# One stream of peer_u for the dense blocks of both passes, and a sixth block gathered wholly

## The chip, the cores and the metric

The kernel runs on one core of one Trainium2 chip: TensorE (PE), VectorE (DVE), ScalarE (ACT), GpSimd (POOL) and SyncE (SP), each with its own program, worked off in order, and 16 DMA engines that they share. The metric is the device time of one execution in microseconds.

## The reference

One layer of a decoder, sequence 1024, width 1024, float32. A token mixer (a gated linear recurrence and a causal convolution, merged and projected) comes first, then the part that the change touches, a product-key expert layer: each token picks 8 x 16 of 16384 experts, expert e being one row of `peer_u` and one of `peer_v`.

```
q = (hf @ w_q).reshape(T, PEER_HEADS, 2, PEER_DQ // 2)
s = jnp.einsum('thpd,hpnd->thpn', q, sub_keys)
sc, idx = lax.top_k(s, PEER_TOPK)
cand = sc[:, :, 0, :, None] + sc[:, :, 1, None, :]          # 256 sums a head
top_sc, pos = lax.top_k(cand, PEER_TOPK)                     # eidx = i * 128 + j of these
gate = jax.nn.softmax(top_sc)
act = gelu(einsum('thkd,td->thk', u_tab[eidx], h))
y = einsum('thk,thkd->td', gate * act, v_tab[eidx])
```

The result is `rms_norm(h + g2 * y)` with a last gain.

## The kernel before

The 1024 tokens are eight blocks of 128. The mixer works on two chunks of four blocks. After a chunk, `ask` makes its queries and top lists, and the expert layer treats its blocks in one of two ways.

*Dense.* All 128 groups of 128 experts are streamed, one group a step. `dots` (L1070) multiplies the group's rows of `peer_u` with the tokens' features into one PSUM tile "ups" and takes gelu of it into `act`; `weigh` (L1088) multiplies that by the dense weights `wgrp`; `add` (L1097) multiplies the weighted result with the group's rows of `peer_v` and sums in six PSUM tiles "y" over all steps. Both tables are float32 and every product is made of three exact ones: `split` (L300) makes a high part on ScalarE (uhi, vhi, whi, L301) and a rest on VectorE (ulo, vlo, wlo, L302). In a step `dots` issues 24 matrix products, and `add` six of 512 columns for each block. Before a block can be weighted densely, `spread` (L960) must build its weights: 128 pairs of one-hot rows and placing products (L982), written to the DRAM tensor `wd`.

*Gathered.* `gather_u` (L925) fetches for each of a token's 128 experts its row of `peer_u` by an indirect DMA on GpSimd's queue (L921, 128 rows, one for each token), and VectorE multiplies and sums it with the tokens' features (L937). `gather_v` (L944) fetches the rows of `peer_v` and VectorE accumulates them (L953). The rows land in tiles "gt": two buffers at first, five once the selection of the last blocks is done.

There are two passes of 128 steps, so each table is streamed twice. Pass one treats blocks 0, 1 and 2; pass two treats blocks 4 and 5 densely and block 6 by halves, its dots gathered and its sum dense. Blocks 3 and 7 are gathered wholly.

The order of the work is made in two ways. `Side` (L82) emits a few steps of the selection (`pick`) and of the gathers at each `tick()`, at rates set by constants; a tick stands after every quarter of `dots` and after each block of `add`. Then a scheduler places each engine's instructions by priority and by its own estimate of times. All loads and stores but the gathers go through SP's queue in that order. A tile pool with `bufs` buffers makes a new tile wait until the one `bufs` before it has been read: `uraw` has two, `vraw` three, "ups" one.

The dense part runs from the first product of `dots` (1616 us) to the last steps in `close` (L1122).

Of the kernel before, what the change touches and what calls it, by code (L numbers as in the profile page):

```python
# [31 lines left out]
PASSES = [([0, 1, 2], 3), ([4, 5, 6], 2)]  # L32
WIDE = 3
DENSE = [b for bs, nu in PASSES for b in bs[:nu]]
MIXED = [b for bs, nu in PASSES for b in bs[nu:]]
GATHERED = [3, 7]
# [5 lines left out]
RATE_GATHER = 0.25  # L42
RATE_PICK_END = 1.1
RATE_GATHER_END = 0.1
HASTE = 1.1
HASTE_LAST = 1.06
HASTE_PICK = 1.2
# [14 lines left out]
GAT_MORE = 3  # L62
VRAW = 3
# [18 lines left out]
class Side:  # L82
    """Work emitted a few steps at a time between the steps of other work, and how urgent it is beside that."""
# [38 lines left out]
def layer_kernel(tc, a, out):  # L122
# [18 lines left out]
    def tick():  # L141
        """A step of the work beside, its vector instructions kept behind the main work of a few steps ago."""
# [21 lines left out]
    with ctx:  # L164
# [41 lines left out]
        def rstd_of(ssq, n, scale, tag):  # L206
            """1 / sqrt(scale * ssq + EPS): a first guess from the exponent, then Newton steps."""
# [13 lines left out]
        # lower bounds of the forget gates  # L221
# [18 lines left out]
        def ada(js, cols=None):  # L240
            """Parts js of the conditioning: as rows in DRAM, or with features on the partitions of cols."""
# [62 lines left out]
        def transpose_split(pp, src, hi, lo, b):  # L304
            """src [tokens, features] -> token block b of hi, lo [feature, k, tokens]."""
# [14 lines left out]
        wd = dram.tile([S // TG, P, NKEYS, TG], F32, name="wd")  # L320

        GQ, GF, GI, GG, GCA, GCB, GGA, GGB = range(8)

        class Mm:
            """Products with streamed weights, 256 columns at a time, in two halves of the contraction."""
# [38 lines left out]
            def weights(self, name, i):  # L364
                """The planned weights that come next; those after them are made ready a product later."""
# [7 lines left out]
            def mm3(self, ps, l, r, step):  # L373
                """ps = sum over k of l(part, k)^T r(part, k) in three exact-product passes."""
# [10 lines left out]
            def feat(self, w, m, act):  # L385
                """Output features 128 m.. on partitions, tokens free."""
# [6 lines left out]
            def halves(self, w, act):  # L393
                """As feat for both m, the first half of the tokens first."""
# [7 lines left out]
            def tok(self, ws, bs, act):  # L402
                """Tokens of block b on partitions, 256 output features, for (w, b) of ws, bs."""
# [617 lines left out]
        def gather():  # L1021
# [4 lines left out]
            for _ in v:  # L1026
                yield
                if picked.keys() >= set(MIXED):
                    break
# [314 lines left out]
```

## Time and profile before

| | |
|---|---|
| three executions | 3749.34, 3755.42, 3763.02 us (median 3755.42) |
| span of the profiled execution, first to last instruction | 3746.1 us (its own time is not listed apart from the span) |
| PE, DVE, ACT, POOL busy | 3610.6 (96%), 3157.9 (84%), 1849.1 (49%), 779.3 us (21%) |
| DMA | 999.44 MB, mean 267 GB/s |
| chain that ended last | PE "y" 4% on each of three lines, "ups" 3% on each of three, others 1% or less |
| pass one | 1616 to 2799 us |
| pass two | 2799 to 3722 us |

Busy time of TensorE counts each matrix product from its start to a modelled end, and products overlap; how fast it works is seen from start to start in the timeline. A share of the DMA engines is the mean over 16 of them. Times in the rows below are from the span's start.

### The profile page before, as it was taken

The numbers are of one execution on the slowest core, as the hardware profiler recorded it, in microseconds if no ns is written. First come the engines' busy times: TensorE is split into PE (matmuls) and PEld (weight loads), VectorE is DVE, ScalarE is ACT, GpSimd is POOL, SyncE is SP. The second block draws the span as 40 slices with busy tenths as digits, with TensorE's granted clock in tenths as the row PEclk, the third lists the DMA queues.
The fourth block names the chain that finished last, engine by engine and source line by source line (L and its number), as shares of the span: only waits on it lengthen the run. The fifth ranks groups of instructions, "written<-read, shape, count | busy, mean of one in ns | idle before, by whom it ended". The sixth has DMA issues, their size and how long they took to land. (4 is left out here: it accounts for less than half of the span.)

```text
span 3746.1 us, 57252 instructions
## 1 busy us (share of the span) xinstructions
PE 3610.6 (96%) x20610; PEld 3203.6 (86%) x20610; DVE 3157.9 (84%) x6739; ACT 1849.1 (49%) x3260; POOL 779.3 (21%) x652
## 2 busy tenths in 40 slices
PE   8999999899999999999999999999998999999997
PEld 5888888778899879988888899999987888888886
DVE  4999989967899966789898888898888888778888
ACT  4111355523467877644444566666534444444443
POOL 0000000000000100013333434343333333233332
PEclk9999999899999999999999999999999999999999
DMA  5222477468444778778788999999999999999996
GB/s 230 79 79 90 152 257 258 168 211 316 164 144 152 241 279 318 270 264 285 261 275 287 345 324 330 332 344 355 332 328 327 328 333 344 316 330 340 328 340 214
DMA packets 371405, 999.44 MB, mean 267 GB/s; under 512 B 30376, under 2 KB 142504, under 8 KB 360112
## 3 DMA queue, kind: packets, MB, share of 16 engines
q1 hardware_dynamic: 278960, 660.19, 50.5%
q0 software_dynamic: 92160, 335.59, 25.3%
q8 instruction: 162, 2.65, 0.3%
q14 instruction: 123, 1.01, 0.1%
HBM read 864.57 MB, written 131.09 MB: 266 GB/s over the span
## 5 line engine op out<-in xcount | busy, mean ns | idle before, releaser
L921 POOL DMA_INDIRECT gt<-in_peer_u_dram,ei x384 | 465.2, 1211 | 2139.1 <-ACT o L759 947.2
L1078 PE MATMUL ups<-u,uhi 128*128 128x384 f32 (+1 forms) x2048 | 637.8, 311 | 12.8 <-ACT act L1086 12.8
L1079 PE MATMUL ups<-u,uhi 128*128 128x384 f32 (+1 forms) x2048 | 636.2, 311 | 2.4 <-DMA u<-u2s 2.4
L1080 PE MATMUL ups<-u,ulo 128*128 128x384 f32 (+1 forms) x2048 | 635.9, 311 | 0.0
L1108 PE MATMUL y<-vhi,whi 128*128 128x512 f32 x1524 | 587.0, 394 | 12.0 <-ACT whi L301 8.0
L1109 PE MATMUL y<-vlo,whi 128*128 128x512 f32 x1524 | 589.9, 393 | 1.6 <-DVE vlo L302 1.5
L937 DVE SCALAR_TENSOR_TENSOR gt<-gt,ut 128x1024 f32<-128x1024 f32 x384 | 466.3, 1219 | 63.9 <-DMA gt<-in_peer_u_dram,ei 58.6
L1112 PE MATMUL y<-vhi,wlo 128*128 128x512 f32 x1524 | 465.7, 392 | 5.9 <-DVE wlo L302 5.9
L301 ACT ACTIVATE uhi<-uraw 128x512 fp32r<-128x512 f32 x512 | 309.9, 625 | 227.0 <-PE ups L1079 177.5
L921 POOL DMA_INDIRECT gt<-in_peer_v_dram,ei x256 | 313.1, 1223 | 515.5 <-DVE yg L953 459.9
L1078 PEld LDWEIGHTS ups<-u,uhi 128*128 128x128 f32 x2048 | 390.0, 190 | 25.6 <-ACT act L1086 16.1
L302 DVE TENSOR_TENSOR ulo<-uraw,uhi 128x512 fp32r<-128x512 f32 x512 | 346.0, 687 | 78.0 <-ACT uhi L301 76.1
L302 DVE TENSOR_TENSOR vlo<-vraw,vhi 128x1024 fp32r<-128x1024 f32 x256 | 312.8, 1222 | 110.8 <-ACT vhi L301 109.8
L1079 PEld LDWEIGHTS ups<-u,uhi 128*128 128x128 f32 x2048 | 390.1, 190 | 12.3 <-DMA u<-u2s 3.1
L1080 PEld LDWEIGHTS ups<-u,ulo 128*128 128x128 f32 x2048 | 389.8, 190 | 0.3
L301 ACT ACTIVATE vhi<-vraw 128x1024 fp32r<-128x1024 f32 x256 | 270.2, 1056 | 234.7 <-PE y L1112 140.7
L1108 PEld LDWEIGHTS y<-vhi,whi 128*128 128x128 f32 x1524 | 287.3, 189 | 68.6 <-ACT whi L301 11.4
L1112 PEld LDWEIGHTS y<-vhi,wlo 128*128 128x128 f32 x1524 | 284.9, 188 | 69.3 <-DVE wlo L302 11.0
L1109 PEld LDWEIGHTS y<-vlo,whi 128*128 128x128 f32 x1524 | 286.4, 189 | 55.2 <-DVE vlo L302 2.4
L953 DVE SCALAR_TENSOR_TENSOR yg<-gt,gate,yg 128x1024 f32<-128x1024 f32 x254 | 324.7, 1278 | 5.6 <-DMA gt<-in_peer_v_dram,ei 5.4
L301 ACT ACTIVATE whi<-wgrp 128x384 fp32r<-128x384 f32 x256 | 133.7, 522 | 352.4 <-DVE wgrp L1091 315.7
L469 DVE SCALAR_TENSOR_TENSOR y<-gl,convw,y 128x1024 f32<-128x1024 f32 x240 | 292.8, 1277 | 0.3
(298 smaller groups left out, 7460.9 us busy)
## 6 DMA issues: line engine op xcount, KB each, us to landing
uraw<-in_peer_uT_dram SPq DMA_DIRECT2D x256, 512.0 KB, 6.4
vraw<-in_peer_v_dram SPq DMA_DIRECT2D x256, 512.0 KB, 6.1
raw<-in_w_in_dram SPq DMA_DIRECT2D x96, 512.0 KB, 5.0
wd<-wt SPq DMA_DIRECT2D x48, 1024.0 KB, 6.7
wgrp<-wd SPq DMA_DIRECT2D x32, 1536.0 KB, 14.0
adaw<-in_ada_w_dram SPq DMA_DIRECT2D x24, 1024.0 KB, 8.1
raw<-in_wq_dram SPq DMA_DIRECT2D x32, 512.0 KB, 5.2
raw<-in_w_b_dram SPq DMA_DIRECT2D x16, 512.0 KB, 4.3
```

What stands on the lines that cost most here:

```text
L301: nc.scalar.activation(hi, src, AF.Copy)
L302: nc.vector.tensor_sub(lo, src, hi.bitcast(F32))
L469: nc.vector.scalar_tensor_tensor(ys[0], gl[:, j:j + S], convw[:, cb, j:j + 1], ys[0], op0=OP.mult, op1=OP.add)
L921: nc.gpsimd.indirect_dma_start(out=gt, out_offset=None, in_=a[table], in_offset=bass.IndirectOffsetOnAxis(ap=ei[:, j:j + 1], axis=0))
L937: nc.vector.scalar_tensor_tensor(gt, gt, 1.0, ut, op0=OP.mult, op1=OP.mult, accum_out=act[:, j:j + 1])
L953: nc.vector.scalar_tensor_tensor(y, gt, w[:, j:j + 1], y, op0=OP.mult, op1=OP.add)
L1078: nc.tensor.matmul(o, hi[:, k], u2[kh][:, 0, k, :m], start=kh + k == 0, stop=False)
L1079: nc.tensor.matmul(o, hi[:, k], u2[kh][:, 1, k, :m], start=False, stop=False)
L1080: nc.tensor.matmul(o, lo[:, k], u2[kh][:, 0, k, :m], start=False, stop=kh + k == 4)
L1108: nc.tensor.matmul(ys[x][dh], whi[:, r], vhi[:, c], start=first, stop=False)
L1109: nc.tensor.matmul(ys[x][dh], whi[:, r], vlo[:, c], start=False, stop=False)
L1112: nc.tensor.matmul(ys[x][dh], wlo[:, r], vhi[:, c], start=False, stop=last)
```

## The change

`peer_u` is streamed once. In each step of pass one, `dots` runs for the blocks of the first pass and again, with the same cut rows, for the blocks of the second; the gelu of the latter goes to the DRAM tensor `ad`, and pass two reads it back, eight steps at a time, as `agrp`. Pass two treats blocks 4 and 5 alone. Block 6 joins 3 and 7 as wholly gathered. The gathers may begin before the other blocks of the chunk are selected, at higher rates; their later buffers are two and two in place of two and three, and `vraw` has two buffers in place of three.

```diff
-PASSES = [([0, 1, 2], 3), ([4, 5, 6], 2)]
+PASSES = [[0, 1, 2], [4, 5]]
-GATHERED = [3, 7]
+GATHERED = [3, 6, 7]
+TICKS = [11, 2]
+LAST_STEPS = 40
-RATE_GATHER = 0.25
+RATE_GATHER = 0.35
-RATE_GATHER_END = 0.1
+RATE_GATHER_END = 0.25
-HASTE_LAST = 1.06
-HASTE_PICK = 1.2
+HASTE_PICK = 2.0
-GAT_MORE = 3
-VRAW = 3
+GAT_MORE = 2
+VRAW = 2
...
+        ad = dram.tile([NKEYS, P, P * len(PASSES[1])], F32, name="ad")
...
+                if not c:
+                    gats.append(ctx.enter_context(tile_pool(name="gat0", bufs=GAT_BUFS, side="right")))
-                for b in sorted(blocks, key=lambda b: (b not in MIXED, b not in GATHERED or c, b)):
+                for b in sorted(blocks, key=lambda b: (b != GATHERED[c], b)):
...
-                if s < end:
+                if s < NKEYS:
                     cut_u[s, kh] = cut(up, raw_u[s][:, 4 * kh:4 * kh + 4], "u", [P, 4, P], 4)
...
-            def dots(s):
+            def dots(s, p):
+                m, off = sizes[p], p * sizes[0]
                 ps = ups.tile([P, n], F32, name="ups")
...
-                acts[s] = dp.tile([P, n // TG, TG], F32, name="act", bufs=AHEAD + 2)
-                nc.scalar.activation(acts[s][:, :m // TG], ps[:, :m].rearrange("p (b t) -> p b t", t=TG), AF.Gelu)
+                if p == 0:
+                    acts[s] = dp.tile([P, n], F32, name="act", bufs=AHEAD + 2)
+                    nc.scalar.activation(acts[s], ps, AF.Gelu)
+                else:
+                    t = dp.tile([P, m], F32, name="actb")
+                    nc.scalar.activation(t, ps[:, :m], AF.Gelu)
+                    nc.sync.dma_start(ad[s], t)
+
+            def kept_acts(s):
+                i = s % NKEYS
+                ag[s // IGRP] = late[0].tile([P, IGRP, sizes[1]], F32, name="agrp")
+                nc.sync.dma_start(ag[s // IGRP], ad[i:i + IGRP].rearrange("i p t -> p i t"))
...
+                act = ag[s // IGRP][:, s % IGRP] if p else acts.pop(s)
+                nc.vector.tensor_mul(w, w, act.rearrange("p (b t) -> p b t", t=TG))
...
+                    gathers[1] = (left - LAST_STEPS) / (TICKS[0] * (NKEYS - 4)) * HASTE if s < 0 else (
+                        left / (TICKS[1] * (NKEYS - 8)) * HASTE)
...
+                if s == NKEYS:
+                    upc.close()
+                    late.append(upc.enter_context(tile_pool(name="bp", bufs=2)))
+                    kept_acts(s)
                 j = s + 4
-                if 0 <= j < end:
+                if 0 <= j < NKEYS:
                     raw_u[j] = up.tile([P, KB, P], F32, name="uraw", bufs=2)
...
-                    dots(s)
+                if 0 <= s < NKEYS:
+                    dots(s, 0)
                 if 0 <= s - AHEAD < end:
                     weigh(s - AHEAD)
-                if 0 <= s - lag < end - 2:
-                    add(s - lag)
+                if blocks and 0 <= s < NKEYS:
+                    add(j, blocks[:2])
+                    blocks = blocks[2:]
+                if 0 <= s < NKEYS:
+                    dots(s, 1)
+                if blocks:
+                    add(j, blocks)
```

In the changed file the products of `dots` stand on L1075 to L1077, those of `add` on L1121, L1122 and L1125, the splits on L300 and L301, the weighing on L1102 and the second gather's sum on L952.

TensorE in the middle of pass one, before. The rows are the end of one step's `dots`, into the PSUM tile ups_20803, and what follows it.

```order
L1078 MATMUL ups_20803<-u21_15345,uhi_20634 128x384
L1079 MATMUL ups_20803<-u21_15345,uhi_20634 128x384
L1080 MATMUL ups_20803<-u21_15345,ulo_20635 128x384
L1108 MATMUL y00_15661<-vhi_21002,whi_20973 128x512
L1109 MATMUL y00_15661<-vlo_21003,whi_20973 128x512
L1108 MATMUL y01_15662<-vhi_21002,whi_20973 128x512
L1109 MATMUL y01_15662<-vlo_21003,whi_20973 128x512
```

TensorE in the middle of pass one of the changed kernel: ups_26082 holds the dots of the first pass's blocks (384 columns), ups_26135 those of the second pass's (256), both in the one buffer.

```order
L1075 MATMUL ups_26082<-u21_15501,uhi_25946 128x384
L1076 MATMUL ups_26082<-u21_15501,uhi_25946 128x384
L1077 MATMUL ups_26082<-u21_15501,ulo_25947 128x384
L1075 MATMUL ups_26135<-u20_15496,uhi_25927 128x256
L1076 MATMUL ups_26135<-u20_15496,uhi_25927 128x256
L1077 MATMUL ups_26135<-u20_15496,ulo_25928 128x256
L1075 MATMUL ups_26135<-u20_15496,uhi_25927 128x256
```

Where the products of `add` followed before, the second 24 of `dots` now follow the first 24, in 98 of the 128 steps; the 18 products of `add` then come after both. In 28 other steps 12 or 6 products of `add` stand between.

VectorE in pass two, before. One step's vlo to the next one's: gt are gathered rows, ulo and wlo rests of splits.

```order
L302 TENSOR_TENSOR vlo_30391<-vraw_30242,vhi_30390 128x1024
L937 SCALAR_TENSOR_TENSOR gt_29716,act_27726<-gt_29716,ut_27724 128x1024
L1091 TENSOR_TENSOR wgrp_29797<-wgrp_29797,act_30212 128x16x16
L302 TENSOR_TENSOR ulo_30190<-uraw_30018,uhi_30189 128x512
L937 SCALAR_TENSOR_TENSOR gt_30237,act_27726<-gt_30237,ut_27724 128x1024
L302 TENSOR_TENSOR ulo_30206<-uraw_30018,uhi_30205 128x512
L302 TENSOR_TENSOR wlo_30360<-wgrp_29797,whi_30359 128x384
L302 TENSOR_TENSOR vlo_30466<-vraw_30314,vhi_30465 128x1024
```

VectorE in the first half of pass two of the changed kernel, the same stretch.

```order
L301 TENSOR_TENSOR vlo_31953<-vraw_31904,vhi_31952 128x1024
L301 TENSOR_TENSOR wlo_31981<-wgrp_31712,whi_31980 128x256
L952 SCALAR_TENSOR_TENSOR yg_28274<-gt_29327,gate7_19444,yg_28274 128x1024
L952 SCALAR_TENSOR_TENSOR yg_28274<-gt_29336,gate7_19444,yg_28274 128x1024
L301 TENSOR_TENSOR wlo_32004<-wgrp_31712,whi_32003 128x256
L301 TENSOR_TENSOR vlo_31976<-vraw_31927,vhi_31975 128x1024
L952 SCALAR_TENSOR_TENSOR yg_28274<-gt_29351,gate7_19444,yg_28274 128x1024
L952 SCALAR_TENSOR_TENSOR yg_28274<-gt_29373,gate7_19444,yg_28274 128x1024
L301 TENSOR_TENSOR wlo_32027<-wgrp_31712,whi_32026 128x256
```

The two ulo of each step are gone, and the weighing stands there for eight steps at once (L1102 ... x8, or in two parts, every eighth step, not in these rows). Two gathered rows stand between one vlo and the next, up to the 56th step of pass two; after it there are none.

## Rows read from the trace of the kernel before

**Rows 1.** Windows: us, busy us (instructions) by engine, clock, DMA share, GB/s

```profile
1240.00:1510.00 270.00, 247.49 (x1664) 227.06 (x1663) 193.51 (x505) 207.59 (x477) 20.59 (x20) 0.96 0.82 287
...
1616.00:2799.00 1183.00, 1155.59 (x6130) 1050.70 (x6129) 1025.90 (x2131) 641.99 (x1254) 428.31 (x345) 1.00 0.90 316
2799.00:3722.00 923.00, 904.87 (x5392) 807.13 (x5391) 757.51 (x1105) 389.75 (x649) 320.12 (x266) 0.99 0.93 327
2800.00:3000.00 200.00, 186.46 (x1089) 164.34 (x1088) 163.38 (x286) 80.78 (x137) 68.18 (x54) 0.98 0.94 332
```

**Rows 2.** Timeline of TensorE, pass one: start us, duration us, what

```profile
2002.16 0.33 PE L1078 MATMUL ups<-u,uhi 128*128 128x384 f32 x1
...
2006.34 0.39 PE L1108 MATMUL y<-vhi,whi 128*128 128x512 f32 x1
...
2008.49 0.39 PE L1108 MATMUL y<-vhi,whi 128*128 128x512 f32 x1
...
2011.22 0.33 PE L1078 MATMUL ups<-u,uhi 128*128 128x384 f32 x1
```

**Rows 3.** Timeline of TensorE, pass two

```profile
3000.14 0.28 PE L1078 MATMUL ups<-u,uhi 128*128 128x256 f32 x1
...
3003.01 0.63 PE L1109 MATMUL y<-vlo,whi 128*128 128x512 f32 x2
```

**Rows 4.** Groups of pass one: what, count, busy us, mean ns, idle

```profile
L982 PE MATMUL gps<-oi,oj 128*128 128x128 f32 x768 | 102.5, 276 | 8.6 <-ACT wt L974 6.5 <-DVE oi L990 2.1
...
L1086 ACT ACTIVATE act<-ups 128x384 f32<-128x384 f32 x128 | 60.6, 474 | 4.2 <-PE ups L1080 4.1
```

**Rows 5.** Timeline of all engines, 2839.8 to 2840.7

```profile
2839.86 0.28 PE L1080 MATMUL ups<-u,ulo 128*128 128x256 f32 x1
...
2840.18 0.38 ACT L1086 ACTIVATE act<-ups 128x256 f32<-128x256 f32 x1 [1.32 <-PE ups L1080]
...
2840.61 0.38 PE L1078 MATMUL ups<-u,uhi 128*128 128x256 f32 x1 [0.47 <-ACT act L1086]
```

**Rows 6.** TensorE's waits, 2799 to 3722: total us, times, longest

```profile
PE ups L1078 <- ACT act L1086: 10.1, 10, 4.2
```

**Rows 7.** Tile gt, 1700 to 2000: ns; who ended idle time, us, times

```profile
L921 POOL DMA_INDIRECT gt<-in_peer_u_dram,ei x77: 939/1148/1906, 1700.8 to 1997.7; - x77
...
  DMA gt<-in_peer_u_dram,ei: 31.8, 29
```

**Rows 8.** The page: queue; costliest groups; issues with KB each

```profile
q0 software_dynamic: 92160, 335.59, 25.3%
...
L921 POOL DMA_INDIRECT gt<-in_peer_u_dram,ei x384 | 465.2, 1211 | 2139.1 <-ACT o L759 947.2
...
L921 POOL DMA_INDIRECT gt<-in_peer_v_dram,ei x256 | 313.1, 1223 | 515.5 <-DVE yg L953 459.9
...
vraw<-in_peer_v_dram SPq DMA_DIRECT2D x256, 512.0 KB, 6.1
...
wgrp<-wd SPq DMA_DIRECT2D x32, 1536.0 KB, 14.0
```

**Rows 9.** Groups of pass two, columns as in rows 4

```profile
L953 DVE SCALAR_TENSOR_TENSOR yg<-gt,gate,yg 128x1024 f32<-128x1024 f32 x141 | 180.3, 1279 | 2.6 <-DMA gt<-in_peer_v_dram,ei 2.5
...
L302 DVE TENSOR_TENSOR vlo<-vraw,vhi 128x1024 fp32r<-128x1024 f32 x128 | 156.7, 1224 | 85.3 <-ACT vhi L301 84.7
...
L301 ACT ACTIVATE vhi<-vraw 128x1024 fp32r<-128x1024 f32 x128 | 135.4, 1057 | 169.5 <-PE y L1112 100.1 <-issue 60.4 <-DMA vraw<-in_peer_v_dram 7.9
...
L1091 DVE TENSOR_TENSOR wgrp<-wgrp,act 128x256 f32<-128x256 f32 x127 | 53.4, 420 | 21.5 <-ACT act L1086 21.2
```

**Rows 10.** Tile vraw, 1700 to 1800, from issue to landing

```profile
DMA to landing us min/median/max: 3.3/4.3/5.4
```

**Rows 11.** Tile vraw, 2799 to 3722, from issue to landing

```profile
DMA to landing us min/median/max: 3.5/6.1/16.2
```

**Rows 12.** Timeline of TensorE at 2903

```profile
2903.47 0.80 PE L1108 MATMUL y<-vhi,whi 128*128 128x512 f32 x1 [3.80 <-ACT vhi L301]
```

More of the change, by code (lines that the diff above doesn't have):

```diff
@@ L564, in turn @@
                     gb = NB * c + b
-                    for n, (blocks, nu) in enumerate(PASSES):
-                        if gb in blocks[:nu]:
+                    for n, blocks in enumerate(PASSES):
+                        if gb in blocks:
                             o = P * blocks.index(gb)
@@ L996, in spread @@
             done.add(b)
-        done, weighed, picked, number, fin, gats = set(), set(), {}, {}, {}, []
+        done, picked, number, fin, gats = set(), {}, {}, {}, []
         def pick(res):
@@ L1021, in gather @@
         def gather():
-            first, later = GATHERED[0], GATHERED[1:]
-            yield from gather_u(first)
-            v = gather_v(first)
[L1026 to L1029, printed above, removed]
-            for b in MIXED:
-                yield from gather_u(b)
-            yield from v
-            for b in later:
+            for b in GATHERED:
                 yield from gather_u(b)
@@ L1039, in dense @@
             n = P * WIDE
+            sizes = [P * len(blocks) for blocks in PASSES]
             lag = AHEAD + LAG
@@ L1049, in dense @@
             nc.sync.dma_start(fin["fg"], bcast_row(a["final_g"], D))
-            raw_u, raw_v, cut_u, cut_v, acts, wg, ws, u2, ys = ({} for _ in range(9))
+            raw_u, raw_v, cut_u, cut_v, acts, wg, ag, ws, u2, ys = ({} for _ in range(10))
+            late = []
             def cut(pool, raw, name, shape, bufs=2):
@@ L1070, in dots @@
-            def dots(s):
-                m = P * PASSES[s // NKEYS][1]
+                    u2[kh] = up.tile([P, 2, 4, sum(sizes)], F32R, name=f"u2{kh}", bufs=1)
+                    o = 0
+                    for p, m in enumerate(sizes):
+                        for x in range(2):
+                            nc.sync.dma_start(u2[kh][:, x, :, o:o + m].bitcast(F32),
+                                              u2s[p, x, :, 4 * kh:4 * kh + 4, :m])
+                        o += m
+            def dots(s, p):
+                m, off = sizes[p], p * sizes[0]
@@ L1287, in layer_kernel @@
         with ExitStack() as fc:
-            blocks = [b for bs, nu in PASSES for b in bs]
-            total = S // P * (1 + HEADS + 1 + 3 * HEADS // SEL + 1) + len(blocks) * (P // 4 + 2)
-            picks[1] = (total - picks[3]) / (7 * (NKEYS - 6)) * HASTE_PICK
+            total = S // P * (1 + HEADS + 1 + 3 * HEADS // SEL + 1) + sum(map(len, PASSES)) * (P // 4 + 2)
+            picks[1] = (total - picks[3]) / (TICKS[0] * (NKEYS - 6)) * HASTE_PICK
             dense(fc, gathers)
```

87 lines of the change are left out of this document (41 added, 46 removed).

## The prediction

> **What bounds the kernel now.** I read the windows by stage first: in both passes of the dense part TensorE is busy nearly all the time (1155.6 of 1183 us, then 904.9 of 923) while the 16 DMA engines are at a share of 0.90 and 0.93 [rows 1]. A busy TensorE is not yet a full one, so I then read its timeline from start to start. A product with 384 columns repeats every 0.174 us (24 of them from 2002.16 to 2006.34, 4.18 us), one with 256 every 0.12 (24 in 2.87 us), and 12 products of 512 columns take 2.73 us [rows 2, 3]. The placing products of the three spread blocks in pass one cost 102.5 us, 34 each [rows 4]. So a pass of before should take 128 x (4.18 + 4.10) + 102.5 = 1162 us and 128 x (2.87 + 4.10) = 892. It took 1183 and 923: 52 us of waits in 2106. TensorE bounds the dense part, with the DMA engines close behind: 327 GB/s at a share of 0.93 is 352 GB/s at a full one, and about 335 at the 0.95 that I allow [rows 1].
>
> **TensorE's own work.** After the change a step of pass one has 24 products of 384 columns, 24 of 256 and 18 of 512: 4.18 + 2.87 + 4.10 = 11.15 us, 1427 us in 128 steps, and with two spread blocks 1495. A step of pass two has 12 products of 512: 2.73 us, 349 in all. That is 1844 where it was 2054, a gain of 210: 175 for the sixth block's 768 products, 35 for its spread. The halved cutting of peer_u and the smaller weighing come off ScalarE and VectorE, which do not set the end in pass one; I count them at nothing. If nothing else moved, the kernel would be 210 us faster. Four things do.
>
> **One bank, two uses (pass one).** There is one PSUM tile "ups". Before, 18 products of the second kind stood between one use of it and the next, time enough for the gelu that empties it. In the new order, in 98 of 128 steps the 24 products for the second pass's blocks stand directly behind the 24 for the first pass's, so the first of them waits for the gelu. The trace has this very pattern: six dots in a row near 2840, the last product at 2839.86, gelu at 2840.18 for 0.38, the next product at 2840.61, which is 0.75 from start to start where 0.12 is usual [rows 5]: 0.63 lost. The gelu is now over 384 columns, 474 ns and not 376 [rows 4], so 0.73 with ScalarE free. Bounds: 0.63; and about 1.27, since the ten such waits after 2799 came to 10.1 us of idle time, one of 4.2 with ScalarE busy elsewhere [rows 6], and a product's drain comes on top. Most of these are of the short kind, so I take 0.78: 98 x 0.78 = 76 us (62 to 124).
>
> **The gathers in pass one.** There are 768 in place of 640. By the new order 79 stand ahead of the dense part (29 before), 576 in pass one (343) and 113 in pass two. In the first 48 steps two buffers serve them and 179 are due, one in 3.2 us. With two buffers the trace ran 77 in 300 us, one in 3.9, and VectorE, which takes its work in order, waited 31.8 us for them [rows 7]. By that rate alone 107 us are lost (698 where the 48 steps have 591); but VectorE waited in only 31.8 of the 300 us, so for the rest something else set that pace. The low end is nothing. In the last 80 steps 397 are due, 4.96 a step; a gather moves 335.59 MB / 640 = 0.524 MB [rows 8], so a step moves 2.60 + 1.05 (512 KB of each table) + 0.20 (an eighth of wgrp) + 0.13 (128 x 256 kept dots) = 3.98 MB, 11.9 us at 335 GB/s: just what TensorE needs with its stall. For both, and the ordinary waits of which the old pass had 21, I take 45 us (10 to 150). Pass one: 1495 + 76 + 45 = 1616.
>
> **Pass two, where the step is short.** vraw has two buffers for three. The load of a row group can start only when VectorE has finished vlo of the group two before, so two steps cannot be shorter than vhi + vlo + landing: 1.06 + 1.22 [rows 9] + 0.2 for four hand-overs of 0.05 (as from the gelu's end to the next product [rows 5]; an estimate) + landing. Landing had a median of 4.3 us between 1700 and 1800, 6.1 in pass two of before, and there 3.5 at best [rows 10, 11]. A step of before lasted 7 us and hid this; a step of 2.73 does not: (2.5 + 3.5) / 2 = 3.0 at best, 3.4 at 4.3, 4.3 at 6.1. SP's queue has the large weight and dots loads between these (1 MB each, every eighth step), and VectorE does eight weighings in one go, so I take a landing of 5: 3.75 us. In the first 56 steps, two gathers stand between one vlo and the next (113 in all): 0.79 (vraw 0.52, weights and dots 0.13 each) + 1.06 = 1.84 MB a step, 5.5 us at 335 GB/s, with VectorE below that at 1.22 + 0.42 + 0.42 + 2 x 1.28 = 4.6 [rows 9]. So 56 x 5.5 + 72 x 3.75 = 578 us where TensorE needs 349. Bounds: 56 x 5.2 (352 GB/s) + 72 x 3.0 = 507, and 56 x 5.9 + 72 x 5 = 690.
>
> The vector and scalar parts of this loop are certain; the landing is the open number. The Trainium skill, "DMA: Bandwidth & Descriptors", section "Anatomy of one DMA — SWDGE (gpsimd) path", gives about 2.0 us and bytes / 436 GB/s for one transfer, 3.2 us for 512 KB as an estimate (its fit is for the other queue). By that a step would be 2.84 us, hardly over TensorE's, and the last 72 steps would save 65 us of my sum. The rows come near it only at their minimum.
>
> **Smaller ones.** At the change of passes the first eight steps' dots are fetched only once the u tiles are free, behind which SP queues vraw loads; four steps of old products, 16 us, cover it: 5 us (0 to 30). The 50 gathers more ahead of the dense part are 65 us of VectorE; between 1240 and 1510 it had 76 us free and TensorE 22 [rows 1]: 8 us (0 to 65). The write of the kept dots stands ahead of the next uraw load on SP, but that load waits for a cut of the same time: nothing (5 at most if the gelu is late).
>
> **Sum.** Dense: 1616 + 5 + 578 = 2199 against 2106, 93 more; with 8 ahead, a span of 3746 + 101 = 3847. What lies around the span is 9 us (median 3755.42 less 3746.1): 3856, say 3855.
>
> **Rivals.**
> (1) Faster: the transfers of pass two are hidden after all. If landing stays so short that TensorE sets the pace of the last 72 steps, and the gathers' bytes flow beside it, pass two is 349 + some 60 and the total 3856 - 170 = 3686. It decides from a pass two under 485 us on. For it: a median of 4.3 in one stretch [rows 10], and loads in pass two are fewer. Against: even the minimum landing gives 3.0 a step, and 1.84 MB in 2.73 us would be 674 GB/s.
> (2) The gathers bind pass one: with two buffers at one in 3.9 us 179 take 698 us, not the 590 that 48 steps have, and with four instead of five VectorE waits again: 3856 + 105 = 3960. For it: the 29 waits of 77 [rows 7].
> (3) The clock falls in pass two. At 2903.47 TensorE had waited 3.80 us, and the windows around it show 0.98 in place of 1.00 [rows 1, 12]. If the pauses of pass two, over 2 us a step at first, bring it to 1.2 GHz for good, 12 products take 5.46 us and the pass 699: 3975. Against: an engine that then works without a pause gets its clock back, as it did there. (The Trainium skill, "TensorE: Matmul & The Clock Gate", section "What's actually happening", says that activity lifts the throttle and idleness restores it; the trace agrees.)
>
> **Chances.** Forecast 0.57, (1) 0.16, (2) 0.12, (3) 0.08, something between forecast and (1) that ends within 0.3% 0.07. A measurement of this kernel tells about 0.3%, 11 us, from no change. Slower by more: 0.57 + 0.12 + 0.08 = 0.77; within: 0.07; faster: 0.16. The range leaves out a tenth at each side: 3705 to 3950. The forecast's own, from the bounds that matter, is 3790 to 3935.
>
> **What would show it.** In the profile after: L1075 waiting for the gelu some hundred times, 70 us or more in all; windows of pass two with TensorE busy for about 60% and VectorE's vhi waits put down to the DMA of vraw; a pass one of about 1616 us and a pass two of about 578. I am wrong if pass two is near 400, if the waits for the gelu are few, or if the gathers make VectorE wait for over 100 us in pass one.

## The result, and the profile after

The changed kernel took 3983.02 us (median of 4 runs, 3976.82 to 3989.88) against 3752.38 for the one before (3745.97 to 3763.02): 1.061 times as long, 95% interval 1.0588 to 1.0632. The forecast was 3855 with a range up to 3950. The direction was right; the size was not, and the time lies beyond the range.

Four landmarks of the profiled execution show where the difference sits (times from the span's start; "pass two" is counted from the last product of `dots` in pass one, so the change of passes is in it, to the last product of `add`; before, where both end within 6 us, to the last product of `dots`).

| | before | forecast | after | after less forecast |
|---|---|---|---|---|
| first product of `dots` | 1616 | 1624 | 1734 | +110 |
| pass one | 1183 | 1616 | 1666 | +50 |
| pass two | 923 | 583 | 571 | -12 |
| from its end to the span's end | 24 | 24 | 13 | -11 |
| span | 3746 | 3847 | 3984 | +137 |

Most of what was missed was lost before the dense part began, on which the prediction spent one sentence. Windows of the changed kernel, cut at its own landmarks (busy us and instructions of each engine, clock, share of the DMA engines, GB/s):

```profile
1240.00:1510.00 270.00, 240.44 (x1492) 216.97 (x1491) 213.82 (x552) 172.85 (x362) 28.78 (x27) 0.91 0.67 242
1510.00:1667.00 157.00, 148.28 (x976) 135.68 (x976) 139.92 (x678) 112.45 (x264) 15.88 (x17) 0.98 0.73 257
1667.00:1734.00 67.00, 35.05 (x171) 31.56 (x170) 43.65 (x173) 47.87 (x119) 8.01 (x7) 0.66 0.79 279
1734.00:3400.00 1666.00, 1542.97 (x8947) 1408.99 (x8948) 1275.40 (x2269) 624.82 (x1189) 698.13 (x571) 0.98 0.86 298
3400.00:3971.00 571.00, 433.99 (x1558) 310.18 (x1556) 404.88 (x566) 187.90 (x265) 145.92 (x112) 0.90 0.82 285
```

The first line answers to the first of [rows 1]: over the same 270 us TensorE was busy 240.4 us, not 247.5, and the granted clock was 0.91, not 0.96, while VectorE had 20 us more to do. The third line has no counterpart in before, where the first dots begin 0.2 us before the last query product is done. Here 67 us lie between the two, in which TensorE was busy for 35 at a clock of 0.66.

What is not in this table lies ahead of it. The stretch from 1070 to 1240 us, in the recurrence, before:

```profile
1070.00:1240.00 170.00, 170.00 (x1243) 159.80 (x1242) 160.51 (x522) 129.13 (x195) 4.54 (x4) 1.00 0.45 151
```

and in the changed kernel, with VectorE's work on gathered rows there (columns as in [rows 4]) and TensorE's two longest waits, of which the kernel before has none in it:

```profile
1070.00:1240.00 170.00, 151.78 (x968) 137.85 (x967) 136.31 (x402) 81.07 (x93) 38.24 (x35) 0.94 0.67 234
...
L937 DVE SCALAR_TENSOR_TENSOR gt<-gt,ut 128x1024 f32<-128x1024 f32 x34 | 41.5, 1220 | 31.4 <-DMA gt<-in_peer_u_dram,ei 31.4
...
PE hps L784 <- DVE o L775: 5.7, 2, 3.0
PE acc L376 <- DVE zg L621: 3.7, 1, 3.7
```

Before, both engines are full there (170.0 and 160.5 us) and two gathers are summed; now 34 are, and they hold VectorE for 41.5 us of work and 31.4 of waiting for their rows. VectorE's first one-hot row of the spread comes at 1349 us and no longer at 1169.

What TensorE did in the 67 us, by groups (columns as in [rows 4]):

```profile
L981 PE MATMUL gps<-oi,oj 128*128 128x128 f32 x160 | 33.6, 389 | 31.3 <-ACT wt L973 14.3 <-ACT oj L991 12.8 <-DVE oi L989 4.2
...
L988 ACT ACTIVATE oj<-iota,tr 128x128 f32<-128x128 f32 x72 | 23.3, 392 | 3.7 <-PE gps L981 3.7
L989 DVE TENSOR_SCALAR oi<-iota,tr 128x128 f32<-128x128 f32 x72 | 20.0, 345 | 10.4 <-PE gps L981 10.3
```

160 records of the placing products of the spread (two to a product, 80 of the 384), 389 ns each where [rows 4] has 276, with 31.3 us of idle time between them: the last groups of the spread, which in before were done under the key scores, ran alone. SP, meanwhile, held the loads of the dense part back. Its queue in that stretch (start us, duration us, what):

```profile
1677.58 0.33 SPq L975 DMA_DIRECT2D wd<-wt  x1
...
1689.88 0.33 SPq L975 DMA_DIRECT2D wd<-wt  x1
1690.25 12.56 SPq L1062 DMA_DIRECT2D u<-u2s  x8
1702.85 2.24 SPq L1186 DMA_DIRECT2D uraw<-in_peer_uT_dram  x2
```

In the kernel before, the same queue had them a hundred microseconds ahead of their use, under the key scores:

```profile
1506.14 0.90 SPq L1068 DMA_DIRECT2D u<-u2s  x2
...
1508.26 1.21 SPq L1068 DMA_DIRECT2D u<-u2s  x2
1509.51 0.49 SPq L1166 DMA_DIRECT2D uraw<-in_peer_uT_dram  x1
```

Here they start at 1690.25, behind a store of `wd`, so that the first rows of `peer_u` were cut at 1712.67: the dots could not have begun much before that even with the spread done.

Pass one: what TensorE and VectorE waited for between 1734 and 3400 (total us, times, longest).

```profile
PE y L1121 <- ACT whi L300: 68.0, 29, 5.8
PE ups L1075 <- ACT act L1085: 45.4, 77, 1.5
```

```profile
DVE yg L952 <- DMA gt<-in_peer_v_dram,ei: 165.9, 109, 6.9
DVE gt L937 <- DMA gt<-in_peer_u_dram,ei: 78.3, 68, 3.7
```

The wait of the dots for the gelu is there, 77 times in the records (ten times in the 923 us of [rows 6]). It comes to 45.4 us where the prediction's sign asked for 70 or more; the table counts idle time, from a product's modelled end, and so less than the prediction's 0.78 from start to start. VectorE stood 244 us for rows of the gathers, where the prediction put its alarm at 100; before, in pass one, 57:

```profile
DVE gt L937 <- DMA gt<-in_peer_u_dram,ei: 54.2, 48, 4.6
DVE yg L953 <- DMA gt<-in_peer_v_dram,ei: 2.9, 4, 1.9
```

Pass two, first two windows (with gathers and without), then TensorE's waits:

```profile
3400.00:3700.00 300.00, 199.53 (x665) 136.24 (x664) 242.64 (x290) 78.34 (x111) 142.51 (x110) 0.87 0.96 345
3700.00:3971.00 271.00, 234.46 (x894) 173.93 (x892) 162.24 (x277) 109.56 (x154) 3.41 (x2) 0.93 0.66 218
...
PE y L1121 <- ACT vhi L300: 95.8, 47, 7.1
PE y L1122 <- DVE vlo L301: 27.8, 35, 2.3
```

and the chain of waits by line, from 3723, where it begins, to 3971 (shares of that stretch):

```profile
by line: DMA vraw<-in_peer_v_dram 46.1%; ACT vhi L300 11.6%; DVE vlo L301 10.3%; issue 7.6%; PE y L1122 5.2%; PE y L1125 4.1%; PE y L1121 3.9%; DMA wgrp<-wd 3.0%; DVE wgrp L1102 1.9%; DVE wlo L301 1.5%; PE y L1148 0.7%; PE y L1149 0.6%; DVE
```

The sums wait for vhi, vhi for the landing of vraw, the landing for VectorE's vlo of two steps before: the loop that the prediction drew. From vlo to vlo, the first 55 steps took 5.6 us each, the rest 3.6.

### The profile page after: what moved, and what is told of

It is laid out like the page before. It is cut to its first block, busy times and chain, and to the rows that moved or that the text cites. A ratio compares the mean times of both kernels' runs of the same rounds, so it can differ in the third digit from the quotient of the medians.

```text
span 3984.0 us, 54734 instructions
## 1 busy us (share of the span) xinstructions
PE 3567.2 (90%) x19583; PEld 3094.4 (78%) x19583; DVE 3123.1 (78%) x6478; ACT 1628.7 (41%) x2807; POOL 936.2 (23%) x780
## 5 line engine op out<-in xcount | busy, mean ns | idle before, releaser
L1075 PE MATMUL ups<-u,uhi 128*128 128x384 f32 (+1 forms) x2048 | 644.2, 315 | 47.5 <-ACT act L1085 45.4
L952 DVE SCALAR_TENSOR_TENSOR yg<-gt,gate,yg 128x1024 f32<-128x1024 f32 x381 | 488.9, 1283 | 190.3 <-DMA gt<-in_peer_v_dram,ei 185.8
L921 POOL DMA_INDIRECT gt<-in_peer_v_dram,ei x384 | 482.8, 1257 | 659.8 <-DVE yg L952 489.0
L1121 PE MATMUL y<-vhi,whi 128*128 128x512 f32 x1272 | 478.6, 425 | 175.1 <-ACT vhi L300 95.8
L1077 PE MATMUL ups<-u,ulo 128*128 128x384 f32 (+1 forms) x2048 | 634.4, 310 | 0.0
L1122 PE MATMUL y<-vlo,whi 128*128 128x512 f32 x1272 | 496.8, 423 | 29.4 <-DVE vlo L301 27.8
L1075 PEld LDWEIGHTS ups<-u,uhi 128*128 128x128 f32 x2048 | 388.6, 190 | 79.6 <-ACT act L1085 70.6
L1121 PEld LDWEIGHTS y<-vhi,whi 128*128 128x128 f32 x1272 | 252.0, 202 | 253.7 <-ACT vhi L300 119.3
L300 ACT ACTIVATE vhi<-vraw 128x1024 fp32r<-128x1024 f32 x256 | 270.8, 1058 | 429.9 <-issue 236.4
L301 DVE TENSOR_TENSOR vlo<-vraw,vhi 128x1024 fp32r<-128x1024 f32 x256 | 313.1, 1224 | 96.3 <-ACT vhi L300 95.7
L1077 PEld LDWEIGHTS ups<-u,ulo 128*128 128x128 f32 x2048 | 388.5, 190 | 0.0
L1125 PE MATMUL y<-vhi,wlo 128*128 128x512 f32 x1272 | 372.9, 405 | 5.0 <-DVE wlo L301 4.9
L1122 PEld LDWEIGHTS y<-vlo,whi 128*128 128x128 f32 x1272 | 251.6, 203 | 112.1 <-DVE vlo L301 65.3
L1125 PEld LDWEIGHTS y<-vhi,wlo 128*128 128x128 f32 x1272 | 249.3, 197 | 60.8 <-DVE wlo L301 7.1
L300 ACT ACTIVATE whi<-wgrp 128x384 fp32r<-128x384 f32 (+1 forms) x256 | 119.7, 468 | 406.9 <-PE y L1122 213.7
L376 PE MATMUL acc<-uhi,whi 128*128 128x512 f32 x640 | 254.2, 398 | 5.6 <-ACT uhi L300 3.6
L378 PE MATMUL acc<-uhi,wlo 128*128 128x512 f32 x640 | 252.5, 395 | 0.0
```

The source lines that it names most:

```text
L300: nc.scalar.activation(hi, src, AF.Copy)
L301: nc.vector.tensor_sub(lo, src, hi.bitcast(F32))
L921: nc.gpsimd.indirect_dma_start(out=gt, out_offset=None, in_=a[table], in_offset=bass.IndirectOffsetOnAxis(ap=ei[:, j:j + 1], axis=0))
L952: nc.vector.scalar_tensor_tensor(y, gt, w[:, j:j + 1], y, op0=OP.mult, op1=OP.add)
L1075: nc.tensor.matmul(o, hi[:, k], u2[kh][:, 0, k, c], start=kh + k == 0, stop=False)
L1077: nc.tensor.matmul(o, lo[:, k], u2[kh][:, 0, k, c], start=False, stop=kh + k == 4)
```

## Experiments

Each is the changed kernel with the edit shown. e2 and e6 leave out the features of blocks 4 and 5, e8 and e9 most of the gathered rows: they show what a part costs and are no kernels to use. First all results (median us; ratio to the kernel before, timed beside each, with its 95% interval; then, from one profiled execution each, the first dots, pass one, pass two):

| | us | ratio | first dots | pass one | pass two |
|---|---|---|---|---|---|
| changed kernel | 3983.02 | 1.061 (1.0588 to 1.0632) | 1734.0 | 1666 | 571 |
| e1_gathers_late | 3968.54 | 1.0573 (1.0535 to 1.061) | 1662.5 | 1664 | 625 |
| e2_u2_small | 3994.98 | 1.0638 (1.0607 to 1.0669) | 1733.5 | 1666 | 584 |
| e3_dots_apart | 4038.83 | 1.075 (1.0714 to 1.0787) | 1743.5 | 1656 | 628 |
| e4_vraw_four | 3875.90 | 1.0311 (1.0276 to 1.0347) | 1735.6 | 1663 | 462 |
| e6_third_buffer | 3980.77 | 1.0604 (1.0576 to 1.0633) | 1740.1 | 1672 | 556 |
| e7_three_mended | 3859.65 | 1.0297 (1.0271 to 1.0323) | 1639.9 | 1670 | 461 |
| e8_few_gathers | 3713.08 | 0.9895 (0.9877 to 0.9913) | 1670.5 | 1576 | 464 |
| e9_few_gathers_apart | 3642.49 | 0.9705 (0.9686 to 0.9723) | 1668.4 | 1494 | 469 |
| e10_rates_kept | 3928.86 | 1.0463 (1.0435 to 1.0492) | 1649.0 | 1686 | 587 |
| e11_five_lines | 3760.92 | 1.0021 (1.0006 to 1.0036) | 1634.1 | 1623 | 487 |
| e13_five_lines_apart | 3748.67 | 0.9988 (0.997 to 1.0005) | 1637.1 | 1574 | 500 |
| e14_rows_together | 3750.23 | 0.9984 (0.9966 to 1.0001) | 1635.9 | 1584 | 502 |

### What delays the dense part

**e1_gathers_late**

```
-RATE_GATHER = 0.35
+RATE_GATHER = 0.25
...
-RATE_GATHER_END = 0.25
+RATE_GATHER_END = 0.1
...
-                if not c:
-                    gats.append(ctx.enter_context(tile_pool(name="gat0", bufs=GAT_BUFS, side="right")))
                 for b in sorted(blocks, key=lambda b: (b != GATHERED[c], b)):
...
-                if c:
-                    gats.append(ctx.enter_context(tile_pool(name="gat1", bufs=GAT_MORE, side="right")))
+                gats.append(ctx.enter_context(tile_pool(
+                    name=f"gat{c}", bufs=GAT_MORE if c else GAT_BUFS, side="right")))
```

> The changed kernel with the two rates of the gathers and the place where gat0 is opened as they were before; all else of the change stays. Theory A: of the 118 us by which the first dots begin later (1616.2 before, 1734.0 after), nearly all come from the 50 or so more gathers that run beside chunk 1's recurrence, norm and key scores (43 us there) and push the last 20 groups of the spread behind the key scores (most of the 67 us between the last query product at 1667.3 and the first dots). Then the first dots begin at 1616 to 1640 us, and the total is 3870 to 3920 us, since the gathers taken out come back beside the dense part. Theory B: the gap of 67 us ahead of the dots is one of room: the dense part's tiles are 16 KB a partition larger and can't be loaded until tiles of the stage before are free. Then only the 43 to 51 us go, the first dots stay at 1680 or later and the total at 3930 or more.

The first dots came at 1662.5: 71.5 of the 118 us, less than theory A said and more than B. The last query product was back at 1625.2 (1667.7 in the changed kernel, 1616.4 before), and all of the spread stood ahead of it. The remaining gap was one wait of TensorE, between 1600 and 1670:

```profile
PE ups L1073 <- ACT uhi L300: 35.4, 1, 35.4
```

The total hardly moved, because the 54 gathers taken from the front (32 issues ahead of the dots, 86 in the changed kernel) went to the end: pass two had 160 for 111 and grew by 54 us.

**e2_u2_small**

```
-                    u2[kh] = up.tile([P, 2, 4, sum(sizes)], F32R, name=f"u2{kh}", bufs=1)
+                    u2[kh] = up.tile([P, 2, 4, sizes[0]], F32R, name=f"u2{kh}", bufs=1)
...
-                    for p, m in enumerate(sizes):
+                    for p, m in list(enumerate(sizes))[:1]:
...
-                m, off = sizes[p], p * sizes[0]
+                m, off = sizes[p], 0
```

> The changed kernel with u2 loaded for three blocks alone (24 KB a partition instead of 40); the second dots take the first blocks' features, so the features of blocks 4 and 5 are left out of the computation, while every product, gelu, gather and store stays. Theory B (room): the loads of u2 go back to where they were, during the key scores, and the first dots begin at 1670 to 1690 us, total 3920 to 3940. Theory A (gathers): the first dots begin within 10 us of 1734 and the total is within 15 us of 3983, since the loads stand in SP's queue behind the stores of the spread, which the gathers make late.

The loads of u2 did go back under the key scores (1556.6 to 1559.7), as theory B wanted, and the first dots still came at 1733.5, as theory A wanted, though not for its reason: the late spread alone fills the gap. Neither theory was whole. e1 takes away the spread and is left with the loads, e2 takes away the loads and is left with the spread.

**e7_three_mended**

e1 and e4 (below), and

```
             up = upc.enter_context(tile_pool(name="up", bufs=2))
+            uc = upc.enter_context(tile_pool(name="uc", bufs=4))
...
-                    cut_u[s, kh] = cut(up, raw_u[s][:, 4 * kh:4 * kh + 4], "u", [P, 4, P], 4)
+                    cut_u[s, kh] = cut(uc, raw_u[s][:, 4 * kh:4 * kh + 4], "u", [P, 4, P], 4)
```

The reason for the second edit is in the addresses that the tiles have in the two programs (bytes of a partition). The pool "up" got 16 KB longer with u2 and now reaches into the tiles of the key scores. It does so with uhi and ulo, which lie at its end; that the pool as a whole, u2 with it, then waits for the key scores is what the edit tests:

```
          pool "up" (u2, uraw, uhi, ulo)      keys of the key scores
before    110240 to 159392                    from 162272
after     104096 to 169632                    from 160736
```

> The changed kernel with three things: the gathers' rates and gat0 as before (e1), four buffers for the streamed rows in pass two (e4), and the cut weights uhi, ulo in a pool of their own above the pool of u2 and uraw, so that u2 and uraw share no room with the tiles of the key scores. Theory of two covers (ahead of the dots stand both the late spread and the late loads of u2; each alone keeps most of the gap): the first dots, at 1734.0 in the changed kernel, 1662.5 in e1 and 1733.5 in e2, now begin at 1618 to 1634 us; pass one stays 1655 to 1670, pass two 465 to 515 with more gathers left for it, total 3765 to 3825. Rival: e1's remaining 37 us come from something other than room (the spread's stores, the weights wgrp): first dots 1650 to 1665, total 3800 to 3855.

The loads of u2 now start at 1515.91 and the first dots at 1639.9, 22.6 us earlier than in e1: the two covers are both real, though the forecast of 1618 to 1634 was missed by 6. What is left is a shorter wait of the same kind (uhi and ulo still lie over the keys), between 1620 and 1660:

```profile
PE ups L1074 <- ACT uhi L300: 12.9, 1, 12.9
```

The total, 3859.65, missed its range of 3765 to 3825: after TensorE's last step 21 gathers were still to be issued, and the span ended 80 us later.

**e10_rates_kept**: e7's pool for uhi and ulo and e1's place for gat0, but the change's rates.

> The changed kernel with gat0 opened where it was before the change and the pool of its own for uhi, ulo (as in e7), but the change's higher rates of the gathers kept: some 59 gathers stand ahead of the dense part (86 in the changed kernel, 32 in e7). If what costs time ahead of the dense part is each gather alike (54 of them made 43 to 51 us up to the last query product): first dots between e7's 1640 and 1734, at 1655 to 1690. If it is only the gathers that begin inside chunk 1's recurrence (before 1233 us) that cost: 1635 to 1650. Total, with two buffers in pass two as in the changed kernel, 3890 to 3950.

The first dots came at 1649.0, at the upper end of the second expectation: 9 us later than e7's, 85 earlier than the changed kernel's (uhi's and ulo's own pool has a part in the 85). The last query product says something else. It came at 1625.2 in e7, at 1645.8 here with 27 gathers more, at 1667.7 in the changed kernel with 27 more again: 21 and 22 us, each gather alike, as the first expectation has it. Some 11 of the 21 fall together with e7's wait for uhi. What comes only with the early opening of gat0 is the late spread: with it gathers run from 1070 us on and the first one-hot row comes at 1349; without it, in e10, at 1181, and all of the spread stood ahead of the last query product.

### Pass two

**e4_vraw_four**

```
-                    raw_v[j] = dp.tile([P, D], F32, name="vraw", bufs=VRAW)
+                    raw_v[j] = late[0].tile([P, D], F32, name="vrawl", bufs=4) if late else dp.tile(
+                        [P, D], F32, name="vraw", bufs=VRAW)
```

> The changed kernel with four buffers instead of two for the streamed rows of peer_v in pass two. Theory 1 (two buffers bind pass two: the next load starts only when VectorE has read the tile before): pass two falls from 571 to 510 to 540 us, total 3920 to 3955. Theory 2 (the transfers bind it: the DMA engines are 0.96 busy at 345 GB/s in its first 300 us, with the gathers): the earlier loads only wait longer for their bytes, pass two 560 to 575 us, total 3970 to 3990.

Pass two fell to 462 us and the total by 107: theory 1, by more than it asked. Windows of e4 in pass two, columns as above:

```profile
3500.00:3600.00 100.00, 86.42 (x349) 63.13 (x348) 88.28 (x113) 40.41 (x58) 46.26 (x29) 1.00 1.04 377
...
3700.00:3800.00 100.00, 85.68 (x345) 62.51 (x345) 90.52 (x119) 40.63 (x57) 40.56 (x24) 1.00 1.04 379
```

and its chain by line over the same stretch as far as it goes, 3723 to 3861:

```profile
by line: PE y L1122 23.6%; PE y L1125 19.2%; PE y L1121 13.8%; DVE vlo L301 13.1%; DMA vrawl<-in_peer_v_dram 6.5%; ACT vhi L300 6.1%; issue 5.5%; DVE wgrp L1102 3.5%; DVE wlo L301 1.7%; PE y L1148 1.3%; DVE ye L1152 0.9%; DVE yg L952 0.9%; 
```

The DMA engines that looked nearly full at a share of 0.96 and 345 GB/s moved 377 to 379 with four buffers, and the chain, led by the loads in the changed kernel, is now led by TensorE's sums; VectorE was busy for 88 to 91 of each 100 us. While gathers ran a step took 3.5 us, with about one gather in it; in the changed kernel 5.6, with two. TensorE still lost 26.4 us once, at the change of passes: SP's queue stood 17.0 us at a load of `wgrp` that waited for VectorE's wlo, and the first kept dots, issued behind it at 3404.85, took 17.5 us to come.

### Pass one

**e3_dots_apart**: by `behind`, which adds a dependency within TensorE's order and no wait, the sums of two blocks are made to follow the last product of `dots(s, 0)` (in `add`), and the first product of `dots(s, 1)` to follow those sums (in `dots`); `mark` notes the product to follow.

```
+                        if kh + k == 0 and p:
+                            behind(n0, 1)
...
+                        if kh + k == 4 and not p:
+                            mark(0)
...
+                        if not p and x < 2:
+                            behind(n0, 0)
...
+                    if not p and x < 2:
+                        mark(1)
```

> The changed kernel with TensorE's order in pass one set to: dots of the first three blocks, sums of two blocks, dots of the other two, sum of the third block; nothing else differs. Theory of the prediction (the one PSUM bank of the dots stalls TensorE 0.75 us where two groups of dots stand back to back, some 98 times, 76 us in all): pass one falls from 1666 to 1590 to 1610 us, the wait of the dots on the gelu nearly goes, total 3905 to 3930. Rival: pass one is held by VectorE with the gathers, and the 76 us come back as waits of the sums on whi (68 us now) and of the dots on their weights: pass one 1645 to 1666, total 3960 to 3985.

On pass one the rival won, though the waits came back on vlo and not, as it had said, on whi. Those of the dots on the gelu went from 45.4 to 7.7 us (1744 to 3400):

```profile
PE y L1141 <- DVE vlo L301: 87.0, 40, 7.9
PE ups L1087 <- ACT actb L1104: 9.5, 10, 4.1
PE ups L1087 <- ACT act L1101: 7.7, 5, 3.2
```

Pass one gained 10 us, issued 29 gathers fewer (542, not 571), and pass two was 57 us longer, with 140 gathers for 111. So the total, 4038.83, lies beyond both ranges.

**e8_few_gathers**

```
-            for j in range(n):
+            for j in range(4):
...
-            for j in range(HEADS * TOPK):
+            for j in range(4):
```

> The changed kernel with 4 instead of 64 rows gathered per token from each table for blocks 3, 6 and 7 (the other rows are left out of the sum); all else stays. It shows pass one and two without gathers beside them. By the prediction's terms (TensorE's own 1495 us, plus 76 of the bank's stall, and nothing else): pass one 1565 to 1585 us. If the stall hides waits that come anyway: 1500 to 1550. If pass one is held by something other than the gathers and the bank: 1600 or more. Pass two with two buffers and no gathers: one step by half of a load, a cut and a subtraction (3.5 + 1.0 + 1.2 us, over two buffers 2.9 us) or by TensorE's 12 products: 360 to 420 us instead of 571. First dots 1640 to 1690.

(A token has 128 rows in each table, not the 64 that the expectation names.) Pass one was 1575.5 us, in the middle of what the prediction's two terms give. The first dots came at 1670.5, so 54 of the 118 us stay with hardly a gather; the order still leaves some spread behind the key scores (40 of 384 products; its first one-hot row comes at 1240), and the pool has the changed kernel's length. Pass two was 464, not 360 to 420: 3.6 us a step with two buffers and hardly a gather. The loads of vraw took 3.4/4.4/6.5 us (least, median, most; 3260 to 3700), and with 4.4 the prediction's loop, (2.5 + landing) / 2, gives 3.45. By the Trainium skill, "DMA: Bandwidth & Descriptors", section "Anatomy of one DMA — SWDGE (gpsimd) path", a transfer of 512 KB would take 3.2 us, an estimate from its fit for the other queue; the trace stays above it.

**e9_few_gathers_apart**: e8 with e3's order.

> The kernel of e8_few_gathers with TensorE's order of e3_dots_apart (some sums between the two groups of dots). If the bank's stall costs what the prediction gave it (76 us) and only the gathers took the gain of e3 away: pass one 1490 to 1515 us, 60 to 80 less than e8. If the order of e3 brings waits of its own (sums ahead of their weights): within 20 us of e8's pass one. Pass two as in e8.

1493.9 us: the bank's stall is worth 82 us when VectorE is free. TensorE's waits in pass one, e8 first (1670 to 3246), then e9 (1668 to 3162):

```profile
PE ups L1075 <- ACT act L1085: 60.2, 95, 5.2
```

```profile
PE ups L1087 <- ACT uhi L300: 8.0, 1, 8.0
PE y L1141 <- DVE vlo L301: 3.3, 3, 1.8
```

Against e8 the gathers cost the changed kernel's pass one 91 us, 72 of them in its first 48 steps (667 us to the gelu of step 48, 595 in e8) and 18 in the other 80. Two buffers served the gathers for 32 of the 48: from 2169 us on, in the 33rd step, more than two are under way at once. By then 35 of the 72 us were lost (423 us to the gelu of step 32, 388 in e8).

**e6_third_buffer**: e2 with `GAT_MORE = 3`.

> The kernel of e2_u2_small (features of blocks 4 and 5 left out) with three buffers instead of two in gat1, as before the change: five lines for the gathers instead of four. Theory G (the gathers hold VectorE in pass one through too few lines: in the changed kernel VectorE waited 162 us on rows of peer_v and 76 us on rows of peer_u there): pass one falls from e2's 1665.5 to 1625 to 1650 us and the total from 3995 to 3950 to 3980. Rival: those waits of VectorE stand in time that TensorE does not need: pass one 1655 to 1668, total 3980 to 4000. The first dots stay at 1725 to 1740 in both.

Pass one took 1672 us, 4 beyond the rival's range and far from theory G's; the total is within the rival's. The third buffer did help at first: to the gelu of step 48 e6 needed 654 us where e2 had 676. The later steps gave it back, and I did not find out where. Two things keep this from being a clean test of five lines: gat1 opens only after 32 steps, and `line()` takes gat0 and gat1 in turn, so that every second gather still has gat0's two buffers. Pass two was 27 us shorter than in e2, which fits more lines for its gathers, though I did not separate that.

**e11_five_lines**

```
-GAT_BUFS = 2
+GAT_BUFS = 3
...
-            ut = gats[0].tile([P, D], F32, name="ut", bufs=1)
+            ut = gats[0].tile([P, D], F32, name="uy", bufs=1)
...
-            y = gats[0].tile([P, D], F32, name="yg", bufs=1)
+            y = gats[0].tile([P, D], F32, name="uy", bufs=1)
...
+                if c:
+                    gats[:] = [gats[0], gats[1], gats[0], gats[1], gats[0]]
```

> The kernel of e7_three_mended with one more line for the gathers from their start on (three in gat0; the tiles ut and yg share one buffer to make room). In e7 21 gathers ran after TensorE's last step and the output ended 80 us after it. If too few lines are what leaves gathers over: none is left over, tail 13 us again, first dots 1640, pass one 1665 to 1690 with some 610 gathers, pass two 455 to 480, total 3785 to 3815. Rival: the lines are not the limit and the extra gathers in pass one hold VectorE and so TensorE for as long: pass one 1700 or more, total 3830 or more.

(The last lines of the edit make three of five gathers in turn use gat0, which now has three buffers.) Better than expected: pass one 1623 us, 47 less than e7 with 32 gathers more in it, none left over at the end, total 3760.92. VectorE's waits for rows in pass one, e7 first (1640 to 3310), then e11 (1634 to 3257):

```profile
DVE yg L952 <- DMA gt<-in_peer_v_dram,ei: 134.2, 98, 7.0
DVE gt L937 <- DMA gt<-in_peer_u_dram,ei: 109.7, 100, 4.2
```

```profile
DVE gt L937 <- DMA gt<-in_peer_u_dram,ei: 71.2, 55, 4.0
...
DVE uy L952 <- DMA gt<-in_peer_v_dram,ei: 42.2, 35, 3.7
```

244 us became 113. The first 48 steps took 634 us for e7's 677.

**e13_five_lines_apart**: e11 with e3's order.

> The kernel of e11_five_lines with TensorE's order of e3 (sums between the two groups of dots). Theory: the bank's stall is worth 82 us where few gathers run (e8, e9) and 10 where they hold VectorE (e3); with five lines VectorE waits less, so a part comes back: pass one 1600 to 1650, pass two 470 to 510 with more gathers left, total 3735 to 3790. Rival: the gathers set pass one's pace and the order only moves waits: pass one 1655 or more, total 3790 to 3830.

Pass one 1574, shorter than expected, 49 less than e11 where e3's order had gained 10. Part of the 49 is 30 gathers fewer in the pass. Total 3748.67: no difference from the kernel before that this measurement could tell.

**e14_rows_together**

```
-        ad = dram.tile([NKEYS, P, P * len(PASSES[1])], F32, name="ad")
+        ad = dram.tile([NKEYS // IGRP, P, IGRP, P * len(PASSES[1])], F32, name="ad")
...
-                    nc.sync.dma_start(ad[s], t)
+                    nc.sync.dma_start(ad[s // IGRP, :, s % IGRP], t)
...
-                nc.sync.dma_start(ag[s // IGRP], ad[i:i + IGRP].rearrange("i p t -> p i t"))
+                nc.sync.dma_start(ag[s // IGRP], ad[i // IGRP])
```

> The kernel of e13_five_lines_apart with the kept dots laid out in DRAM in the order in which a group of eight is read (8 KB in a row for a partition in place of 1 KB). In e4 the first such load took 17.5 us and TensorE waited 26.4 us at the change of passes. If the short rows make it slow: that wait falls to 10 us or less, pass two 12 to 25 us shorter than e13's, total 3715 to 3775. Rival: the load is slow because transfers of other queues are ahead of it: within 6 us of e13.

Pass two 502 for e13's 500: the layout of the kept dots does not matter here. But there was little to gain: e13 waits 12.3 us at the change of passes (e14 11.3) and not e4's 26.4. So the pair does not tell why the first group took 17.5 us in e4.

## Why the prediction was wrong in size

**The step that failed** is the one under "Smaller ones": "The 50 gathers more ahead of the dense part are 65 us of VectorE; between 1240 and 1510 it had 76 us free and TensorE 22 [rows 1]: 8 us (0 to 65)". It measured 118. It went wrong in three ways.

- It weighed the gathers in a stretch where most of them did not run. 57 more stood ahead, not 50, and between 1240 and 1510 there were 6 more (26, before 20). 34 were summed between 1070 and 1240, for which the prediction read no row, and there neither engine had room: TensorE was busy for 170.0 of 170 us, VectorE for 160.5. They took 41.5 us of VectorE's work and 31.4 of waiting for rows, a wait that the 65 us leave out, and TensorE lost 18 us to waits for VectorE and others. The last products of the recurrence went from 1322 to 1376 us, and e1 brought them to 1332. Nor was the idle time after 1240 free: e10 has ten gathers more than e7 between 1240 and 1400 (26, 16), and its recurrence ends 16.5 us later (1348.9, 1332.4).
- It did not ask what is late next. VectorE's one-hot rows for the spread, which is work beside, began 180 us later (1349, before 1169), so that a part of it was pushed out from under the key scores and ran alone at a clock of 0.66: with e1 this and the first point are 71.5 us.
- It did not ask where u2 for five blocks would lie. The longer pool shares room with the key scores' tiles, so the loads came behind them: 22.6 us by e7 against e1. This cover was hidden behind the other (e2). About 24 us remain in e7, half of them the wait for uhi; the rest stays open.

**Gathers in pass one**: the right mechanism, mis-sized. 45 us were given, 91 measured (e8), within the bounds of 10 to 150. The two buffers were named, for 48 steps (it was 32), with 107 us by the rate alone; the value taken was too near the low end. Rival (2) asked for 105 us more in pass one than the forecast; 50 came. Its mechanism is there, at half its price.

**TensorE's own work and the bank's stall**: 1495 and 76 us forecast, 1494 (e9) and 82 (e8 less e9) measured. Where the second group of dots follows the first directly, 76 times in the changed kernel's records, the switch takes 0.92 us from start to start, 0.75 more than a product; 0.78 were given. What the prediction did not see is that the two terms don't simply add: while VectorE stands for gathers, e3 got back 10 us of the 82.

**Pass two**: 583 forecast, 571 measured, and the last steps, 3.75 forecast, took 3.6, with e8 the same. The first 55 steps took 5.6 us each, forecast 5.5. But those were costed by bytes at 335 GB/s, and for that the agreement is in part luck: the 352 GB/s at a full share, from which the 335 come, is no ceiling, since e4 passed as many gathers at 377 GB/s beside four buffers, and the pass was 109 us shorter. What held it were two buffers and the gathers together. Either alone takes off some 108 us: four buffers beside the gathers (e4, 462 us), or two with hardly a gather (e8, 464).

**Rivals (1) and (3)**: pass two under 485 us was not reached with two buffers beside the gathers, but it was with four (462). The clock did not stay low: 0.87 and 0.93 in the two windows of pass two, and 1.00 in e4 from 3500 on, where TensorE was busy for 86 of each 100 us. (The Trainium skill, "TensorE: Matmul & The Clock Gate", section "What's actually happening", has activity lift the throttle; the trace agrees: 0.66 ahead of the dots, 0.98 in pass one.)

**Where the gain went.** With hardly a gather, e9 is at 0.9705 of the kernel before. How much of the 3% are the fewer products is not shown, since no run leaves out the 640 gathers of the kernel before. What the 128 gathers more and the room they were not given took is seen from the mends. Four mends (gathers as late as before, a pool of its own, four streamed buffers, five lines) bring 3983 to 3761, and the order of e13 to level with the kernel before, not past it.

## What to carry to other kernels

Price added work in the stretch where the new order puts it, with the waits for its data, and not where the old kernel has idle time; then ask which work beside is pushed out and where it ends. Before a tile grows or a buffer count falls, look up which tiles of the stage before it shares its room with and how long a step the remaining buffers must hide. A share of the DMA engines near one does not show that bytes are the limit: look at whether the next load was already waiting.

## What the runs showed of the hardware

The DMA engines moved 377 to 381 GB/s for 300 us with streamed loads and gathers mixed (e4; the changed kernel 345). With up to four loads under way beside the gathers, 512 KB landed in 7.0 us (median) where e8, with two and hardly a gather, had 4.4: each transfer took longer and more was moved. The placing products took 389 ns in place of 276 at a granted clock of 0.66, that is with two thirds of the stretch at 1.2 GHz and the rest at 2.4 (1 - 0.68 / 2); TensorE had been busy for 35 of its 67 us.
